# Spreading the first pair's preparation over three windows of projections, and moving the head sums ahead of the inversion's matmuls in their slot

## The chip, the cores and the metric

The kernel runs on one core of one Trainium2 chip. The metric is the device time of one execution in microseconds, the median over several runs. Times inside an execution come from one profiled run; they are counted from the start of its span.

## The reference

Two layers over 256 tokens and 2048 channels. Each layer projects the normalised input once and feeds two groups of 16 heads: a bidirectional RWKV-7 scan and windowed attention. Both are gated, joined, projected back and added to the residual. The change touches only the RWKV-7 half, whose arithmetic is, cut down:

```python
h = rms_norm(x, norm_g[l])
proj = h @ w_in[l]                       # split, and the rw part shifted between neighbours
kk = heads(kf * k_k); kk = kk * rsqrt(max(sum(kk * kk, -1), 1e-24))
for d, rev in enumerate((False, True)):
    w = -softplus(-(w0[d] + tanh(xw) @ decay_up[d])) - 0.5
    decay = exp(-exp(w))
    a = sigmoid(a0[d] + xa @ iclr_up[d])
    kd = heads(kf * (1 + (a - 1) * k_a))
    y = y + wkv_scan(rh, heads(decay), kd, vh, kk, heads(a), rev)
    bonus = bonus + sum(rh * kd * r_k, -1)
out = group_norm(y) * lnx_g + lnx_b + bonus * vh
...
x = x + concat([y_rw * silu(g_rw), y_at * silu(g_at)]) @ w_out[l]
```

## The kernel before

**Projections as a stream.** All projections of a layer are one stream of steps (class `Stream`). A step is three matmuls on TensorE (lines 286 to 288: the weights' high part with the input's high and low part, the weights' low part with the input's high part). A 128-column projection takes 16 steps. Its weights arrive in two halves by DMA, and each half is split on the fly: ScalarE writes the high part (`hi`, line 216), VectorE the low part (`lo`, line 218). The results lie in two PSUM tiles `pm` taken in turn and are evacuated by VectorE and ScalarE (lines 413 to 426).

**Windows and slots.** A layer's RWKV-7 heads are worked on in eight pairs. `window(64, ...)` runs 64 steps, the four projections of one pair (k, v, r, gate), in 14 slots of four or five steps; ahead of the steps of a slot it advances the chains of earlier pairs that are listed for that slot. Windows are counted from w = 0 in each layer, where window w projects pair w. A chain is a Python generator; one advance issues the instructions up to its next `yield`. The chains of a pair are

- `scan_p`, the preparation: low-rank products (`pza`), cumulative decay (`lw`), the sum of squares over a head (`pk`, line 654) and its reciprocal (`kd`), the scaled keys and queries (`mv`, `bk`), and the bonus `bv`, which needs a second head sum (`pbn`, line 654) over two vector operations on `lw`;
- `scan_i`, the inversion of the 64x64 blocks by doubling: masks (`pg`, line 746, then `ge`, line 752), transposes (`pt`, evacuated by ScalarE into `bt`, line 782, and four copies into `suv`, line 787), then for each level products `pq` (line 837 for the first level, 847 for the others), their evacuation `QF`, products `pd` (853, 855) and two predicated copies into `tv` and `tt` (856, 857); at the end `pf` and `pn`;
- `scan_b`, the scan over the four chunks.

In the kernel before, pair p has its preparation in window p+1, its inversion in all 14 slots of window p+2 and the first two of p+3, and its scan in p+3 and p+4. The preparation has nine parts, in slots 4 to 11 and 13 of its window, one part each. In one slot the chains are advanced in the order scan, inversion, preparation.

**What sets the order.** TensorE runs in the order of the program text (`manual_schedule`). VectorE and ScalarE get a fixed order from a planner, which puts a ready instruction by its priority: the place in the program, moved up by 40 for `lo` and by 95 for `scan_b`. Operations issued through `PA` and `PV` keep the program's order among themselves on their engine; their line in the profile is that of the helper, 231. The short-lived PSUM tiles `pza`, `pk`, `pg`, `pt`, `pq`, `pd`, `pbn`, `pf`, `pn` share one pool of two buffers of two banks each (`wpair`); a new tile takes a buffer whose last reader is done.

In the first layer `setup` also runs in window 0: it reduces the angles of the rotary positions on VectorE in a long chain (lines 340 to 359) and takes two sines on ScalarE (line 358).

Of the kernel before, what the change touches and what calls it, by code (L numbers as in the profile page):

```python
# [21 lines left out]
T = 256  # L22
# [19 lines left out]


SLOTS = 14
STAGE_P = [4, 5, 6, 7, 8, 9, 10, 11, 13]
STAGE_I = (list(range(SLOTS)), [0, 1])
STAGE_B = (list(range(1, 14)), [1, 2, 3, 4])
ATT = [
# [81 lines left out]
def hybrid_trunk_kernel(ctx, tc, xT, wi, wv, wo, par, fing, dup, iup, sink, pos, cst, out):  # L130
# [17 lines left out]
    def wpair(name):  # L148

        return ps_w.tile([128, 2, 512], F32, tag="w", name=name)  # L150

    def wbank(name):
        return wpair(name)[:, 0]

    def st(tag, shape, dt=F32, bufs=1):
        return sp.tile([128, *shape], dt, tag=tag, name=tag, bufs=bufs)
# [475 lines left out]
    def layer(l):  # L632
# [14 lines left out]
        def low_rank(o, w, x):  # L647
            PE.matmul(o, w[0], x[0], start=True, stop=False)
            PE.matmul(o, w[0], x[1], start=False, stop=False)
            PE.matmul(o, w[1], x[0], start=False, stop=True)  # L650

        def head_sums(o, x):
            for r in half:
                PE.matmul(o[r, 0:T], bones[r, r], x[r, 0:T], start=True, stop=True)
# [3 lines left out]
        def scan_p(p, t):  # L658
            K, VV, R, iu, du = t["k"], t["v"], t["r"], t["iu"], t["du"]
            dd = lambda x: x.rearrange("p (d x) -> p d x", d=2)  # L660
            two = lambda x: x.unsqueeze(1).to_broadcast([128, 2, T])
            c8 = lambda x: x.rearrange("p (n j) -> p n j", j=64)

            pza = wpair("pza")
            pz, pa = pza[:, 0], pza[:, 1]
            for d in range(2):
                low_rank(pz[:, d * T : (d + 1) * T], [a[0 : RANK + 1, d, :] for a in du], [a[0 : RANK + 1] for a in L.TW])
            LW = st("lw", [2 * T])
            for d in range(2):
                low_rank(pa[:, d * T : (d + 1) * T], [a[0:RANK, d, :] for a in iu], [a[0:RANK] for a in L.XA])  # L670
            PA.activation(LW, pz, AF.Tanh, scale=0.5)
            TH = st("th", [2 * T])
            for d in range(2):
                PA.activation(TH[:, d * T : (d + 1) * T], pa[:, d * T : (d + 1) * T], AF.Tanh, scale=0.5, bias=dpm(NSH + 16, d * 8 + p))
            sq = st("t1", [T], bufs=3)
            PA.activation(sq, K, AF.Square, scale=prm(P_KK, p))
            KR = st("kkr", [T])
            PA.activation(KR, K, AF.Identity, scale=prm(P_KK, p))
            yield

            PV.tensor_scalar(LW, LW, 1.0, None, op0=ALU.add)
            msk = MSK.rearrange("p c j -> p (c j)")
            for x in (LW[:, 0:T], LW[:, T : 2 * T][:, ::-1]):
                PV.tensor_tensor_scan(x, msk, x, 0.0, op0=ALU.mult, op1=ALU.add)
            yield
            pk = wbank("pk")
            head_sums(pk, sq)
            PP = st("pp", [2, NC, 64])
            IP = st("ip", [2, NC, 64])
            PA.activation(PP.rearrange("p d c j -> p (d c j)"), LW, AF.Exp, scale=DECAY_C)  # L690
            PA.activation(IP.rearrange("p d c j -> p (d c j)"), LW, AF.Exp, scale=-DECAY_C)
            KD = st("kd", [T])
            PV.reciprocal(KD, pk[:, 0:T])
            PV.scalar_tensor_tensor(KD, KD, 1e24, KR, op0=ALU.min, op1=ALU.mult)
            yield

            MV = st("mv", [2, NC, 2, 64], bufs=3)
            BK = st("bk", [2, NC, 3, 64])
            km = st("lw", [2 * T])
            kr4 = KR.rearrange("p (c j) -> p c j", j=64)  # L700
            PV.scalar_tensor_tensor(MV[:, 0, :, 0, 1:64], PP[:, 0, :, 0:63], -1.0, kr4[:, :, 1:64], op0=ALU.mult, op1=ALU.mult)
            PV.scalar_tensor_tensor(MV[:, 1, :, 0, 0:63], PP[:, 1, :, 1:64], -1.0, kr4[:, :, 0:63], op0=ALU.mult, op1=ALU.mult)
            PA.activation(MV[:, 0, :, 0, 0:1], kr4[:, :, 0:1], AF.Copy, scale=-1.0)
            PA.activation(MV[:, 1, :, 0, 63:64], kr4[:, :, 63:64], AF.Copy, scale=-1.0)
            PA.activation(km, TH, AF.Identity, scale=dpm(NSH, p), bias=dpm(NSH + 8, p))
            yield
            PV.scalar_tensor_tensor(dd(TH), dd(TH), 1.0, two(KD), op0=ALU.add, op1=ALU.mult)
            BK8 = BK.rearrange("p d c s j -> p (d c) s j")
            IP8 = IP.rearrange("p d c j -> p (d c) j")
            PV.scalar_tensor_tensor(BK8[:, :, 1, :], c8(TH), 0.5, IP8, op0=ALU.mult, op1=ALU.mult)  # L710
            yield
            PV.tensor_tensor(dd(km), dd(km), two(K), op=ALU.mult)
            PV.tensor_tensor(BK8[:, :, 2, :], c8(km), IP8, op=ALU.mult)
            PA.activation(BK8[64:128, :, 0, :], BK8[64:128, :, 2, :], AF.Copy)
            yield
            PV.tensor_tensor(
                MV[:, :, :, 1, :], R.rearrange("p (c j) -> p c j", j=64).unsqueeze(1).to_broadcast([128, 2, NC, 64]), PP, op=ALU.mult
            )
            PC = st("pc", [2, NC], bufs=3)
            PA.activation(PC[:, 0, :], PP[:, 0, :, 63], AF.Copy)  # L720
            PA.activation(PC[:, 1, :], PP[:, 1, :, 0], AF.Copy)
            yield


            PV.tensor_tensor(km[:, 0:T], km[:, 0:T], km[:, T : 2 * T], op=ALU.add)
            PV.scalar_tensor_tensor(km[:, 0:T], km[:, 0:T], prm(P_RK, p), R, op0=ALU.mult, op1=ALU.mult)
            yield
            pb = wbank("pbn")
            head_sums(pb, km)
            bv = st("bv", [T], bufs=3)  # L730
            PV.tensor_tensor(bv, pb[:, 0:T], VV, op=ALU.mult)
            t.update(BK=BK, MV=MV, PC=PC, bv=bv)
            yield


# [230 lines left out]
        def scans(w):  # L966

            gens = []
            for lag, scan, at in ((4, scan_b, STAGE_B[1]), (3, scan_i, STAGE_I[1]), (3, scan_b, STAGE_B[0]), (2, scan_i, STAGE_I[0]), (1, scan_p, STAGE_P)):
                p = w - lag  # L970
                if 0 <= p < NP:
                    if (scan, p) not in chains:
                        chains[scan, p] = scan(p, L.ts[p])
                    gens.append((chains[scan, p], at))
            return gens
# [73 lines left out]
        for w in range(NP + 2):  # L1049
            window(64, *scans(w), *([(setup_, [2, 5])] if l == 0 and w == 0 else []))  # L1050
        att = attend()
        window(64, *scans(NP + 2), (att, ATT[0]))
        window(64, *scans(NP + 3), (att, ATT[1]))
        window(64, (att, ATT[2]))
        for _ in att:
# [124 lines left out]
```

## Time and profile before

| | |
|---|---|
| median of 3 runs | 1224.29 us (1222.6 to 1225.03) |
| the profiled execution | 1220.4 us, of which its span 1218.6 us |
| TensorE (PE) busy | 1177.0 us, 97% of the span |
| VectorE (DVE) busy | 929.5 us, 76% |
| ScalarE (ACT) busy | 747.6 us, 61% |
| GpSimd (POOL) busy | 19.1 us, 2% |
| DMA | 166.72 MB, mean 137 GB/s |
| mean granted TensorE clock | 0.992 of full speed |

A busy share is an average over stages with different limits. The line "waits" of an engine tells how long it stood still and which engine's instruction let it go on; a row of the timeline has the start, the length, engine, line and tiles of an instruction or of a run of equal ones, and in brackets the idle time ahead of it. In a table by stretches each row has the length of a stretch, each engine's busy time in it with the count of instructions, the granted clock (PEclk, 1.00 is full speed), the DMA share and GB/s.

In layer 0, window 0 starts at 27.8 us, window 1 at 50.4, window 2 at 85.1 and window 3 at 122.3; in layer 1 they start at 623.8, 646.4, 679.8 and 716.9. Windows 4 to 7 take 42.1 us each in both layers.

### The profile page before, as it was taken

To read this page: it belongs to the slowest core of one execution; us is meant where nothing else is said; L and a number is where in the kernel's file an instruction comes from. 1 tells how busy PE (TensorE), PEld (TensorE's weight loads), DVE (VectorE), ACT (ScalarE), POOL (GpSimd) and SP (SyncE) were. 2 spreads that over 40 slices of the span, in tenths; PEclk is the share of its full clock that TensorE was granted. 3 is DMA by queue.
4 is the path that set the end of the run, shared out by engine and by line. 5 is a ranking of instruction groups with operands and counts; after the bars stand their busy time and mean duration, and the time that the engine had idled before them with its cause. 6 is when DMAs were issued, how large, how long until landed. Compare 5 with 4: busy or idle time off the path is not lost. (4 is left out here: it accounts for less than half of the span.)

```text
span 1218.6 us, 38161 instructions
## 1 busy us (share of the span) xinstructions
PE 1177.0 (97%) x16204; PEld 1092.3 (90%) x16204; DVE 929.5 (76%) x2067; ACT 747.6 (61%) x1840; POOL 19.1 (2%) x23
## 2 busy tenths in 40 slices
PE   7989999999999999999999899999999999999996
PEld 6978998999898889999999788989999888899996
DVE  7978878888877668866677788878887866786554
ACT  6656665766666557655555556766676565675553
POOL 0000000000000000000000000000000000000000
PEclk9999999999999999999999999999999999999998
DMA  7533233323323433477654333233233334345653
GB/s 252 177 129 125 95 112 111 107 96 116 119 89 102 134 111 132 141 242 237 205 189 163 111 121 114 86 107 126 90 112 106 115 101 133 125 142 177 208 191 123
DMA packets 60411, 166.72 MB, mean 137 GB/s; under 512 B 7728, under 2 KB 22736, under 8 KB 60240
## 3 DMA queue, kind: packets, MB, share of 16 engines
q1 hardware_dynamic: 60240, 164.27, 40.5%
q8 instruction: 127, 2.08, 0.7%
q14 instruction: 44, 0.36, 0.1%
HBM read 157.43 MB, written 4.19 MB: 133 GB/s over the span
## 5 line engine op out<-in xcount | busy, mean ns | idle before, releaser
L286 PE MATMUL pm<-XH,hi 128*128 128x256 f32 x1664 | 497.0, 299 | 8.1 <-ACT XH L179 5.9
L216 ACT ACTIVATE hi<-raw 128x512 fp32r<-128x512 f32 x560 | 328.4, 624 | 247.8 <-PE pm L287 173.6
L288 PE MATMUL pm<-XH,lo 128*128 128x256 f32 x1664 | 470.1, 282 | 3.2 <-DVE lo L218 3.2
L287 PE MATMUL pm<-XL,hi 128*128 128x256 f32 x1664 | 469.7, 282 | 0.1
L218 DVE TENSOR_TENSOR lo<-raw,hi 128x512 fp32r<-128x512 f32 x560 | 368.5, 687 | 89.8 <-ACT hi L216 83.0
L286 PEld LDWEIGHTS pm<-XH,hi 128*128 128x128 f32 x1664 | 315.7, 190 | 33.8 <-issue 13.4
L288 PEld LDWEIGHTS pm<-XH,lo 128*128 128x128 f32 x1664 | 316.2, 190 | 4.5 <-DVE lo L218 4.0
L287 PEld LDWEIGHTS pm<-XL,hi 128*128 128x128 f32 x1664 | 316.5, 190 | 0.7 <-DVE XL L180 0.7
L286 PE MATMUL pm<-MH,hi 128*128 128x256 f32 x512 | 144.0, 281 | 0.0
L287 PE MATMUL pm<-ML,hi 128*128 128x256 f32 x512 | 143.8, 281 | 0.0
L288 PE MATMUL pm<-MH,lo 128*128 128x256 f32 x512 | 143.8, 281 | 0.0
L286 PEld LDWEIGHTS pm<-MH,hi 128*128 128x128 f32 x512 | 96.6, 189 | 0.8 <-issue 0.8
L287 PEld LDWEIGHTS pm<-ML,hi 128*128 128x128 f32 x512 | 96.6, 189 | 0.0
L288 PEld LDWEIGHTS pm<-MH,lo 128*128 128x128 f32 x512 | 96.6, 189 | 0.0
L920 ACT ACTIVATE suv<-pcc 64x128 f32<-64x128 f32 x128 | 34.2, 267 | 20.4 <-PE pq L847 14.4
L856 DVE CAST_PREDICATED tv<-LV,pd 128x256 f16<-128x256 uint8 x80 | 34.5, 431 | 13.6 <-PE pd L855 13.1
L849 ACT ACTIVATE QF<-pq 128x256 f16<-128x256 f32 x80 | 30.9, 386 | 20.8 <-PE pq L847 20.0
L752 DVE TENSOR_TENSOR ge<-pg,C 128x1024 f32<-128x1024 f32 x32 | 39.1, 1222 | 5.0 <-PE pg L746 5.0
L904 ACT ACTIVATE rh<-pcc 128x128 f32<-128x128 f32 x64 | 17.5, 273 | 35.3 <-PE pcc L902 34.9
L1005 ACT ACTIVATE mv<-mv,mx 128x257 f32<-128x257 f32 x64 | 31.8, 502 | 11.6 <-DVE mx L1002 11.6
L746 PE MATMUL pg<-mv,bk 64*128 64x128 f32 x512 | 37.2, 285 | 0.0
L857 DVE CAST_PREDICATED tt<-LV,pd 128x256 f16<-128x256 uint8 x80 | 34.1, 426 | 0.0
(240 smaller groups left out, 1849.9 us busy)
## 6 DMA issues: line engine op xcount, KB each, us to landing
raw<-wi SPq DMA_DIRECT2D x207, 512.0 KB, 3.4
raw<-wo SPq DMA_DIRECT2D x64, 512.0 KB, 3.8
raw<-wv SPq DMA_DIRECT2D x8, 512.0 KB, 3.2
rrot<-u SPq DMA_DIRECT2D x80, 32.0 KB, 1.9
vg<-xT SPq DMA_DIRECT2D x16, 128.0 KB, 5.2
xd<-vg SPq DMA_DIRECT2D x16, 128.0 KB, 2.4
vg<-xd SPq DMA_DIRECT2D x16, 128.0 KB, 3.5
g<-dup SPq DMA_DIRECT2D x16, 97.0 KB
```

The source lines that it names most:

```text
L216: A.activation(hi[:, q], raw[:, q], AF.Copy)
L218: V.tensor_tensor(lo[:, q], raw[:, q], hi[:, q].bitcast(F32), op=ALU.subtract)
L286: PE.matmul(pm, wh, rh[:, kk, :], start=(kk == 0), stop=False)
L287: PE.matmul(pm, wh, rl[:, kk, :], start=False, stop=False)
L288: PE.matmul(pm, wl, rh[:, kk, :], start=False, stop=(kk == 15))
L746: PE.matmul(pg[:, h, c * 128 : (c + 1) * 128], BK[half[h], d, c, 1 - h : 3 - h, :].rearrange("p s j -> p (s j)"), MV[half[h], d, c].rearra ...
L752: V.tensor_tensor(GEd(d), pg.rearrange("p h (c x) -> p h c x", c=NC), gm[d].unsqueeze(1).unsqueeze(1).to_broadcast([128, 2, NC, 128]), op= ...
L849: A.activation(t_sub(QF), flat4(pq[:, :, 0:128]), AF.Copy)
L856: V.copy_predicated(t_sub(TC), t_mask, flat4(pd[:, :, 0:128]))
L857: V.copy_predicated(v_sub(TT), v_mask, flat4(pd[:, 0, 128:384].rearrange("p (d x) -> p d x", d=2)))
L920: A.activation(here(h), pc[half[h], 1], AF.Copy)
L1005: A.activation(Sc[:, h, q, 0:257], Sc[:, h, q, 0:257], AF.Exp, scale=0.125, bias=mx[:, q : q + 1], accum_out=den[:, q : q + 1])
```

## The change

The preparation gets two more `yield`s, one behind each of its head sums, and so has eleven parts: part 3 is the sum `pk` alone, part 10 the sum `pbn` alone; `BK`, `MV` and `PC` are handed on behind part 8, and `bv` behind part 11.

For pairs 1 to 7 parts 3 and 10 are advanced in slots 6 and 13 ahead of the inversion's part of the same slot, all others in the slots as before behind it. The set of instructions in each slot is the same as before.

For pair 0 the parts are spread: 1 and 2 in slots 12 and 13 of window 0; part 3 in slot 3 of window 1, 4 in slot 3 behind it, 5, 6, 7, 8 in slots 5, 6, 8, 10; part 9 in slot 1 of window 2, part 10 in slot 3 ahead of the inversion's first `pq`, and part 11 (`bv`) in slot 3 behind it.

```diff
-STAGE_P = [4, 5, 6, 7, 8, 9, 10, 11, 13]
+STAGE_P = (([6, 13], [4, 5, 6, 7, 8, 9, 10, 11, 13]),)
+STAGE_P0 = (([], [12, 13]), ([3], [3, 5, 6, 8, 10]), ([3], [1, 3]))
...
             pk = wbank("pk")
             head_sums(pk, sq)
+            yield
...
+            t.update(BK=BK, MV=MV, PC=PC)
             yield
...
             pb = wbank("pbn")
             head_sums(pb, km)
-            bv = st("bv", [T], bufs=3)
+            yield
+            t["bv"] = bv = st("bv", [T], bufs=3)
             PV.tensor_tensor(bv, pb[:, 0:T], VV, op=ALU.mult)
-            t.update(BK=BK, MV=MV, PC=PC, bv=bv)
             yield
...
-            for lag, scan, at in ((4, scan_b, STAGE_B[1]), (3, scan_i, STAGE_I[1]), (3, scan_b, STAGE_B[0]), (2, scan_i, STAGE_I[0]), (1, scan_p, STAGE_P)):
+            prep = [(lag, at) for lag, at in enumerate(STAGE_P0) if lag == w] + [(1, at) for at in STAGE_P if w > 1]
+            stages = [(4, scan_b, STAGE_B[1]), (3, scan_i, STAGE_I[1]), (3, scan_b, STAGE_B[0])]
+            stages += [(lag, scan_p, at[0]) for lag, at in prep]
+            stages += [(2, scan_i, STAGE_I[0])]
+            stages += [(lag, scan_p, at[1]) for lag, at in prep]
+            for lag, scan, at in stages:
```

## The prediction

> **What bounds the kernel now.** I read the page's busy shares first, then TensorE's list of waits, then the timeline at the longest wait, then tables by stretches.
>
> ```profile
> PE 1177.0 (97%) x16204; PEld 1092.3 (90%) x16204; DVE 929.5 (76%) x2067; ACT 747.6 (61%) x1840; POOL 19.1 (2%) x23
> ...
> PE pbn L654 <- DVE lw L231: 8.2, 2, 4.1
> PE pq L847 <- DVE tv L856: 5.8, 4, 1.6
> PE pk L654 <- ACT t L231: 1.6, 1, 1.6
> ...
> 758.60:800.60 42.00, 41.92 (x756) 38.08 (x754) 35.13 (x75) 28.08 (x74) 1.01 (x1) 1.00 0.32 107
> ```
>
> TensorE is the bound: 97% busy, and in a full window (window 4 of layer 1, the last row) 41.92 of 42.00 us. Work taken off VectorE or ScalarE there is worth nothing; only TensorE's waits can be won. The longest group is the second head sum `pbn` behind the two vector operations on `lw`: two waits of 4.1 us, one in each layer. The only `pk` wait is 1.6 us. The timeline shows where the first `pbn` wait lies and what follows it.
>
> ```profile
> 79.94 0.65 PE L654 MATMUL pbn<-lw,C 64*64 64x256 f32 x4 [4.11 <-DVE lw L231]
> 80.52 0.51 PE L286 MATMUL pm<-XH,hi 128*128 128x256 f32 x1
> ...
> 83.60 0.41 PE L288 MATMUL pm<-XH,lo 128*128 128x256 f32 x1
> ...
> 85.52 0.28 PE L286 MATMUL pm<-XH,hi 128*128 128x256 f32 x1
> 85.64 0.28 PE L287 MATMUL pm<-XL,hi 128*128 128x256 f32 x1
> ...
> 27.80:50.40 22.60, 22.60 (x192) 22.60 (x193) 20.58 (x51) 13.11 (x26) 0.00 (x0) 1.00 0.54 183
> 50.40:62.00 11.60, 11.15 (x95) 10.94 (x93) 9.77 (x25) 10.75 (x16) 0.00 (x0) 1.00 0.48 148
> 62.00:75.80 13.80, 12.65 (x100) 11.80 (x100) 13.42 (x24) 10.07 (x22) 0.00 (x0) 1.00 0.46 156
> 75.80:79.90 4.10, 0.03 (x1) 0.00 (x0) 3.92 (x9) 1.47 (x5) 0.00 (x0) 1.00 0.51 156
> 79.90:84.00 4.10, 4.07 (x21) 3.49 (x21) 0.42 (x1) 0.11 (x1) 0.00 (x0) 0.59 0.28 111
> 84.00:94.00 10.00, 10.00 (x129) 9.17 (x129) 6.68 (x12) 6.07 (x13) 0.00 (x0) 1.00 0.27 87
> ...
> 646.40:674.60 28.20, 23.40 (x195) 22.48 (x193) 23.37 (x43) 16.34 (x35) 0.00 (x0) 1.00 0.49 161
> 674.60:679.70 5.10, 5.07 (x35) 4.13 (x35) 1.20 (x3) 1.01 (x2) 0.00 (x0) 0.67 0.23 81
> ```
>
> Both `pbn` waits lie at slot 13 of window 1, where pair 0 is prepared and no inversion lengthens the window. VectorE is then the slow engine: 13.42 of 13.8 us busy ahead of the wait and 3.92 of 4.1 in it. The wait has a second price. Behind it 14 matmul starts take 83.60 - 80.52 = 3.08 us, 0.22 each, where 0.12 is the pace later (85.52 to 85.64); the granted clock is 0.59 for 4.1 us. Lost: 4.1 x 0.41 = 1.7 us. In layer 1 the clock is 0.67 for 5.1 us: 5.1 x 0.33 = 1.7 again. So each `pbn` wait costs 4.1 + 1.7 = 5.8 us. The 1.6 us `pk` wait lies in the stretch 62.0 to 75.8, whose clock is 1.00: it costs only itself.
>
> **The change part by part.** No instruction is added or removed on any engine. No moved part issues a DMA or a GpSimd instruction, so SP's and POOL's queues keep their work.
>
> *What goes.* In window 1, `pk` comes a whole window part after its squares (made in slot 12 of window 0): its wait goes, -1.6. `pbn` moves to slot 3 of window 2, two slots behind the two operations it waits for, which lie in slot 1 at VectorE's head: -5.8 in each layer. Sum: -13.2 us.
>
> *Moved low-rank products.* The twelve `pza` matmuls move from window 1 to window 0 and cost TensorE the same in either place. Their inputs are made between slots 0 and 9 of window 0, so I price a new wait at nothing; if that cover went, the price would be that of the `pk` wait, 1.6.
>
> *The new wait in window 2.* This is the one cost that the rows of the kernel before already show.
>
> ```profile
> 92.23 0.33 PE L837 MATMUL pq<-tv,AB 64*64 64x32 f16 x10
> ...
> 87.87 1.23 DVE L752 TENSOR_TENSOR ge<-pg,C 128x1024 f32<-128x1024 f32 x1 [0.56 <-PE pg L746]
> ...
> 90.44 1.15 ACT L216 ACTIVATE hi<-raw 128x512 fp32r<-128x512 f32 x2
> 91.50 0.79 ACT L782 ACTIVATE bt<-pt 128x768 f32<-128x768 f32 x1
> 92.30 1.55 ACT L787 ACTIVATE suv<-pt 64x256 f32<-64x256 f32 x4
> ...
> 182.87 0.63 PE L654 MATMUL pk<-t,C 64*64 64x256 f32 x4
> ...
> L231 DVE SCALAR_TENSOR_TENSOR lw<-lw,PR,kr 128x256 f32<-128x256 f32 x16 | 7.8, 485 | 0.6
> L231 DVE TENSOR_TENSOR lw<-lw 128x256 f32<-128x256 f32 x16 | 6.7, 420 | 0.0
> L231 DVE TENSOR_TENSOR bv<-pbn,vg 128x256 f32<-128x256 f32 x16 | 6.7, 420 | 2.1 <-PE pbn L654 2.1
> ```
>
> Today the first `pq` of pair 0 starts at 92.23, in the buffer that the second `pg` left. After the change `pbn` takes that buffer, and `pq` needs one of two others: that of `pt`, free when the last `suv` copy ends (92.30 + 1.55 = 93.85), or `pbn`'s own, free after `bv`. A head sum takes about 0.6 us (the `pk` row), so TensorE stands ready for `pq` at 92.23 + 0.6 = 92.8. Through `pt` the wait is 1.0 us; through `bv` it is 0.42 plus handing over, some 0.5. If the two `lw` operations (0.42 + 0.49) slip ahead of the second mask `ge`, the copies behind it come 0.9 later: 1.9. So 0.5 to 1.9; I take 1.0, the value with today's order, in each layer: +2.0. Queued behind the waiting `pq` are the window's steps. The second lateness of this chain follows at 115.51:
>
> ```profile
> 115.51 0.30 PE L847 MATMUL pq<-tv,AB 64*64 64x32 f16 x16 [1.63 <-DVE tv L856]
> ```
>
> There TensorE waits for VectorE's backlog, which a TensorE one microsecond later would shorten. I leave it as it is, and count up to 1.6 per layer as a possible gain.
>
> *VectorE's reserve in layer 0.* With the waits gone TensorE covers 27.8 to 79.9 (52.1 us) in 52.1 - 4.1 - 1.6 = 46.4. VectorE's work there is 20.58 + 9.77 + 13.42 + 3.92 = 47.7 us, less the 0.9 that moves to window 2. So in layer 0 it hardly keeps up, and some 2 to 3 us of splits and evacuations go over into window 2. There 84.0 to 94.0 holds 6.68 of 10.0 us of work and gets 0.42 + 0.49 + 0.42 = 1.3 more: 6.7 + 1.3 + 2.5 = 10.5 in 10. I put the cost at +1.0, between 0 and 2.6 (47.7 + 1.3 - 46.4, all of it on the path). In layer 1 no setup runs; VectorE has 23.37 of 28.2 busy in window 1, and I charge nothing.
>
> *The head sums in the other windows.*
>
> ```profile
> 185.79 0.30 PE L853 MATMUL pd<-QF,tt 64*64 64x32 f16 x16
> ...
> 184.51 1.76 DVE L231 RECIPROCAL kd<-pk 128x256 f32<-128x256 f32 x1
> ...
> 203.87 0.42 DVE L857 CAST_PREDICATED tt<-LV,pd 128x256 f16<-128x256 uint8 x1
> 204.20 0.42 DVE L231 TENSOR_TENSOR bv<-pbn,vg 128x256 f32<-128x256 f32 x1
> ...
> 204.34 0.30 PE L863 MATMUL pf<-tv,NEYE 64*64 64x256 f16 x4
> ```
>
> An earlier `pk` gives nothing: it ends at 183.50, and the reciprocal starts only at 184.51, when VectorE comes to it. What it could cost is a buffer. The reciprocal ends at 186.27, 0.48 after the next `pd` starts at 185.79; `bv` ends at 204.62, 0.28 after `pf` starts. If `pd` and `pf` must now take the head sums' buffers, a window loses 0.48 + 0.28 = 0.76 us. If they take the buffer of the `pq` or `pd` that they follow, which they wait for in any case, nothing. In the program of the kernel before, a tile takes whichever buffer is free, and one `pd` takes the one that its own `pq` has just left. So 0 to 0.76 per window; I take 0.
>
> *Sum:* -13.2 + 2.0 + 1.0 = -10.2 us. The profiled execution (1220.4, span 1218.6) would come to 1210.2; against the median shown, 1224.29 (3.9 above that execution), I predict 1214.1.
>
> **A rule that speaks against the change.** In layer 0 the moved part's tanh comes close to the setup's two sines on ScalarE.
>
> ```profile
> 51.66 1.28 ACT L358 ACT_TABLE_LOAD   x1
> 52.95 0.42 ACT L358 ACTIVATE SIN<-SIN 128x256 f32<-128x256 f32 x1
> ```
>
> A table load takes 1.28 us here, the sine starting 1.29 after it. ScalarE is busy 10.75 of 11.6 us in that stretch, so each extra change of tables would reach TensorE through late `hi` splits. If the planner sets the tanh among the sines, two more changes cost 2 x 1.29 = 2.6 us: 1214.1 + 2.6 = 1216.7.
>
> The Trainium skill, ScalarE: Activation LUTs, What ACT_TABLE_LOAD costs, puts a switch at 1283 ns of load and some 1380 ns of drain. The trace agrees on the load and shows no drain between load and sine; by the page two switches would be 5.3 us and the time 1219.4.
>
> **The rivals.**
>
> *VectorE keeps the pace.* The stalls leave window 1 and come back in part at `pg` and `pq` of window 2: the reserve costs 2.6, the new wait 1.9 in both layers. -13.2 + 3.8 + 2.6 = -6.8: 1217.5. For it: 47.7 us of work in 46.4. Against: layer 1 has room.
>
> *The reorder takes it back.* The head sums' buffers hold `pd` and `pf` in all fourteen windows of pairs 1 to 7: 14 x 0.76 = +10.6 on -10.2: 1224.7, no change. For it: only two buffers, both overtakings are in the rows above. Against: another buffer is always free by then.
>
> *Slower.* As before, but the new plan also sets the reciprocal one split later:
>
> ```profile
> L218 DVE TENSOR_TENSOR lo<-raw,hi 128x512 fp32r<-128x512 f32 x560 | 368.5, 687 | 89.8 <-ACT hi L216 83.0
> ```
>
> 14 x (0.76 + 0.69) = +20.3: 1224.3 - 10.2 + 20.3 = 1234.4. It decides from 10.2 / 14 = 0.73 us per window on. Against: it needs a wrong buffer and a worse order at once, in a stage that now has no wait.
>
> **How the numbers follow.** Forecast 0.57, tables 0.05, VectorE's pace 0.18, taken back 0.10, slower 0.10. A change under 0.2% (2.4 us) can't be told from none. Faster 0.57 + 0.05 + 0.18 = 0.80, same 0.10, slower 0.10. The range starts at 1209: -13.2, the new waits at 0.5 each (+1.0) and both 115.51 waits gone (-3.2) give -15.4, 1208.9. It ends at 1221, above the VectorE and table cases, leaving out the last two. The forecast's own range is 1209 to 1217.
>
> **What would show it.** Right: no `pbn` or `pk` wait over 0.3 us, a clock of 1.00 in window 1 of both layers, a new wait of 0.5 to 1.9 us at line 837 in window 2, and full windows still at 42 us. Wrong: waits at `pg` in layer 0 of over 2 us, waits of `pd` for the reciprocal or of `pf` for `bv`, or full windows of over 42.5 us.

## Result and the profile after

| | before | after |
|---|---|---|
| median | 1224.49 us (1222.6 to 1225.03) | 1215.89 us (1214.87 to 1218.23) |
| ratio | | 0.9935, 95% interval 0.9917 to 0.9953 |
| the profiled execution | 1220.4 us, span 1218.6 | 1214.87 us, span 1213.1 |

The change makes the kernel 8.6 us faster by the medians; predicted were 10.2 us and 1214.1 us. (The median before has one run more here than in the table ahead of the prediction, 1224.29 us.) Line numbers of the changed kernel are two to four higher: the head sums are line 656, the first `pq` 841, the later ones 851.

The page's busy shares of the changed kernel, and three of the larger groups of its TensorE waits (total, count, longest):

```profile
PE 1175.4 (97%) x16204; PEld 1096.0 (90%) x16204; DVE 928.4 (77%) x2067; ACT 747.5 (62%) x1840; POOL 19.1 (2%) x23
...
PE pq L851 <- DVE tv L860: 5.6, 5, 1.6
PE pm L290 <- DVE lo L220: 4.2, 6, 1.3
PE pq L841 <- ACT suv L791: 3.3, 2, 2.2
```

The work is the same. The `pbn` and `pk` waits are gone, and a new group stands there: the first `pq` of pair 0 waiting for the copies out of `pt`, once in each layer. The table by stretches (length, PE, PEld, DVE, ACT, POOL, then clock) shows where the time went:

```profile
28.10:52.20 24.10, 24.08 (x204) 24.08 (x205) 22.14 (x55) 14.98 (x31) 0.00 (x0) 1.00 0.52 176
52.20:78.00 25.80, 24.40 (x200) 23.10 (x198) 23.18 (x49) 18.51 (x35) 0.00 (x0) 1.00 0.46 160
78.00:89.10 11.10, 8.87 (x104) 7.74 (x104) 8.12 (x14) 7.63 (x14) 0.00 (x0) 1.00 0.44 145
645.50:669.00 23.50, 23.50 (x200) 22.85 (x198) 20.90 (x40) 14.40 (x31) 0.00 (x0) 1.00 0.55 184
...
758.60:800.60 42.00, 41.92 (x760) 38.42 (x758) 35.12 (x75) 28.00 (x74) 1.01 (x1) 1.00 0.33 107
```

Window 1 of layer 1 (645.5 on) now has TensorE busy throughout at full clock, where it stood 4.8 us before. In layer 0 it still loses 1.4 us (24.40 of 25.80 busy). The full window is as before, 41.92 of 42.00. By the first projection matmul of each window, windows 0 and 1 together shrink from 57.3 to 50.9 us in layer 0 and from 55.9 to 48.7 in layer 1, and window 2 grows from 37.2 to 40.0 and 40.4.

### The profile page after: what moved, and what is told of

Its sections match the earlier page's. It is cut to its first block, busy times and chain, and to the rows that moved or that the text cites. A ratio compares the mean times of both kernels' runs of the same rounds, so it can differ in the third digit from the quotient of the medians.

```text
span 1213.1 us, 38155 instructions
## 1 busy us (share of the span) xinstructions
PE 1175.4 (97%) x16204; PEld 1096.0 (90%) x16204; DVE 928.4 (77%) x2067; ACT 747.5 (62%) x1840; POOL 19.1 (2%) x23
## 5 line engine op out<-in xcount | busy, mean ns | idle before, releaser
L851 PE MATMUL pq<-tv,AB 64*64 64x32 f16 x1280 | 33.6, 186 | 6.4 <-DVE tv L860 5.6
L750 PE MATMUL pg<-mv,bk 64*128 64x128 f32 x512 | 37.2, 285 | 0.0
```

What stands on the lines that cost most here:

```text
L750: PE.matmul(pg[:, h, c * 128 : (c + 1) * 128], BK[half[h], d, c, 1 - h : 3 - h, :].rearrange("p s j -> p (s j)"), MV[half[h], d, c].rearra ...
L851: PE.matmul(narrow(pq[:, d], h ^ d, c), hq(AB, d, c, h), sub(TC, h, d, c, d * b), start=True, stop=True)
```

## Experiments

All times are medians; they were taken in three sets, each beside the kernel before. It had 1223.2 us beside the first three runs below and the bank of its own, 1224.1 beside the two windows, the sum in slot 0, the run without the angles and the first run with raised copies, and 1222.4 beside the last two. Runs of different sets are compared by their ratios.

**The changed kernel once more.** No edit.

> The changed kernel once more, beside the others on the same chip, so that differences of 1 to 3 us can be read. Every theory expects 1213 to 1218 us, 6 to 11 us below the kernel before. On the clock: the theory that one 3.4 us stretch of the clock's grid, about half idle, is enough to halve the clock expects the 1.6 us waits at the later pq (window 2 and window 9) to be followed by a 0.5 stretch in some executions and not in others, by where they fall; the theory that only an idle time of over 3.4 us does it expects no 0.5 stretch between 20 and 1200 us in any execution without a wait that long.

Measured: 1215.47 us, ratio 0.993 (0.9918 to 0.9942). As expected in time. On the clock the second theory falls: this profile has half clock for 3.41 us from 90.9 and from 995.5 us, each behind a stretch with 2.1 and 1.9 us of idle time and no longer wait. The last section has more.

**The order in the slot alone.**

```diff
-prep = [(lag, at) for lag, at in enumerate(STAGE_P0) if lag == w] + [(1, at) for at in STAGE_P if w > 1]
+prep = [(1, at) for at in STAGE_P]
```

> Pair 0's preparation stays whole in window 1 (slots 4 to 11 and 13, as before); only the order in the slot is changed, head sums ahead of the inversion. Main theory (the gain is the spreading of pair 0): 1224.5 us, within 2 us of the kernel before, both pbn waits of 4.1 us still there with a clock of 0.5 behind each, full windows at 42.0 to 42.1 us. Rival (the order in the slot is worth something in the full windows): 1218 or less, full windows below 41.8. Second rival (the order costs through the shared buffers, 0.76 us a window): 1235.

Measured: 1224.51 us, ratio 1.0003 (0.9993 to 1.0013). Its TensorE waits and a full window:

```profile
PE pbn L656 <- DVE lw L233: 8.2, 2, 4.1
...
758.60:800.60 42.00, 41.92 (x756) 38.41 (x756) 35.14 (x75) 28.12 (x73) 1.01 (x1) 1.00 0.32 107
```

Both long waits stand as before, and the full window is the same to 0.01 us. The order is worth nothing, and the buffers take nothing for it.

**The spreading alone.**

```diff
-STAGE_P = (([6, 13], [4, 5, 6, 7, 8, 9, 10, 11, 13]),)
+STAGE_P = (([], [4, 5, 6, 6, 7, 8, 9, 10, 11, 13, 13]),)
```

> Pair 0 is spread over three windows as in the changed kernel; pairs 1 to 7 keep their head sums behind the inversion's part of the slot, as before. Main theory: the same as the changed kernel, 1215.9 us, within 1.5 us; the pf wait at the start of window 9 in layer 0 back from 0.8 to 0.4 us. Rival (half of the gain is the order): 1220.

Measured: 1215.72 us, ratio 0.9934 (0.9921 to 0.9947). All of the gain is the spreading of pair 0. The `pf` wait is 0.54 us here and 0.45 with the order alone, and 0.78 and 1.43 in the two profiles of the changed kernel, so it doesn't follow the order.

**Two windows instead of three.**

```diff
-STAGE_P0 = (([], [12, 13]), ([3], [3, 5, 6, 8, 10]), ([3], [1, 3]))
+STAGE_P0 = (([], []), ([6], [4, 5, 6, 7, 8, 9, 10]), ([3], [1, 3]))
```

> Pair 0's parts 1 to 8 stay in window 1 (slots 4 to 10, the first head sum ahead in slot 6); only the bonus, parts 9 to 11, moves to window 2 as in the changed kernel. It tells whether the early start in window 0 is needed. Theory A (the bonus sum's late inputs were the whole trouble): the pbn waits and the half clock behind them are gone, the pk wait of 1.4 to 1.6 us in layer 0 is back, the pq waits of 2.2 and 1.0 us in window 2 stay: 1217.5 us. Theory B (VectorE is the slow engine of window 1, so the lateness only moves on): pg in window 2 waits for mv or bk by 1 to 3 us in layer 0 and under 1 in layer 1: 1219 to 1221.

Measured: 1216.86 us, ratio 0.9939 (0.9925 to 0.9952). Its waits:

```profile
PE pq L841 <- ACT suv L791: 2.6, 2, 1.3
...
PE pk L656 <- ACT t L233: 1.4, 1, 1.4
...
89.07 0.21 PE L841 MATMUL pq<-tv,AB 64*64 64x32 f16 x3 [1.30 <-ACT suv L791]
```

Theory A: no `pbn` wait, no `pg` wait, the `pk` wait back. Moving only the bonus, three of eleven parts, gives nearly all of the gain. The early start in window 0 is worth 0.5 to 1.1 us by the ratios (0.9939 against 0.9935 and 0.993), which the intervals don't separate. VectorE's lateness did not move on to `pg`. One part of theory A missed: the `pq` waits are 1.3 us in both layers, not 2.2 and 1.0. So the longer wait of layer 0 comes only with the early start; by the first projection matmul windows 0 and 1 of layer 0 take 50.9 us with it and without it, those of layer 1 48.7 and 49.5.

**A bank of its own for the moved sum.**

```diff
-pb = wbank("pbn")
+pb = ps_c.tile([128, 512], F32, tag="y", name="pbn") if p == 0 else wbank("pbn")
```

> As the changed kernel, but the second head sum of pair 0 is written to a PSUM bank that the scan uses only from window 3 on, so that the first pq of the inversion finds the buffer of the second pg free. Main theory (that pq waits for the copies out of pt only since pbn took its buffer: 2.2 us in layer 0 and 1.0 in layer 1): no wait over 0.3 us at line 841, 3.2 us less, 1212.7 us; if the later waits for tv grow in turn, 1214. Rival (pq waits for the mask and the ScalarE copies AB behind it, whatever the buffer): the waits stay and the time too, 1215.9.

Measured: 1210.28 us, ratio 0.9893 (0.9879 to 0.9908). The first groups of its waits, in order of size:

```profile
PE pm L288 <- ACT XH L181: 6.6, 1, 6.6
PE pq L851 <- DVE tv L860: 6.3, 5, 1.6
PE pm L290 <- DVE lo L220: 3.1, 6, 1.0
PE pm L288 <- ACT hi L218: 2.3, 2, 1.7
```

No wait is left at line 841, so the buffer was its cause. The gain over the changed kernel, 5.2 us, is 2 us more than the 3.3 us of waits, and more than was expected. In two of three profiles with the 2.2 us wait (the changed kernel again, and the spreading alone) a half-clock stretch stood behind it; the last section shows one. That the other 2 us lie there is not shown: the profile with the bank of its own has three half-clock stretches between 20 and 1190 us, those of the changed kernel two each.

**The moved sum in slot 0.**

```diff
-STAGE_P0 = (([], [12, 13]), ([3], [3, 5, 6, 8, 10]), ([3], [1, 3]))
+STAGE_P0 = (([], [12, 13]), ([3], [3, 5, 6, 8, 10, 12]), ([0], [0]))
```

> As the changed kernel, but pair 0's part 9 lies in slot 12 of window 1 and its second head sum in slot 0 of window 2 ahead of pg, bv behind it. Theory (the pq wait is a matter of which PSUM buffer pbn takes): pq waits under 0.3 us at line 841; pbn may wait up to 1 us in layer 0, where VectorE is late, and 0 in layer 1: 1211 to 1213 us. Rival (pbn so early meets VectorE's lateness again): pbn waits 2 us or more in layer 0 and pg's second half waits for bv: 1216 or more.

Measured: 1217.82 us, ratio 0.9954 (0.9937 to 0.9971).

```profile
PE pbn L656 <- DVE lw L233: 3.6, 2, 2.6
```

Line 841 waits no more, as the theory had it, but the rival is right on `pbn` and on the time: `pbn` waits 2.6 us in layer 0 and 1.0 in layer 1. The rival's wait of `pg` for `bv` does not show. The sum stands two slots behind its two operations here too (slot 12 to slot 0; slot 1 to slot 3 in the changed kernel), so the distance alone does not do it: at the end of window 1 the sum stands behind VectorE again. It wants a place where VectorE has had time and a free buffer at once.

**Without the rotary angles in layer 0.** The sine and cosine tables are set to constants.

```diff
-        ang = st("g", [T], bufs=2)
-        ...
-        V.tensor_scalar(SIN, SIN, C[:, C_OFF["sgn"] : C_OFF["sgn"] + 1], None, op0=ALU.mult)
+        V.memset(SIN, 0.0)
+        V.memset(COS, 1.0)
```

> The changed kernel without the first layer's chain of rotary angles: the sine and cosine tables are set to constants, so the attention half computes something else. It tells what VectorE's and ScalarE's load by that chain costs in layer 0. Theory (layer 0 loses by VectorE's lack of reserve and by table loads): in layer 0 the waits for hi and lo in window 1 (1.4 us together) go and the first pq wait falls from 2.2 to the 1.0 us of layer 1, windows 0 to 2 of both layers get within 0.7 us of each other: about 2.6 us less than the changed kernel, 1213. Rival (the layers differ by something else): under 1 us less, pq wait still over 2.

Measured: 1210.74 us, ratio 0.9895 (0.988 to 0.9911). The first `pq` of layer 0 (its line numbers are 20 lower here):

```profile
85.70 0.33 PE L821 MATMUL pq<-tv,AB 64*64 64x32 f16 x11 [1.01 <-ACT suv L771]
```

The wait is that of layer 1 to 0.01 us, and no wait for `hi` or `lo` over 0.3 us is left in window 1. Those two account for 2.6 us. The medians differ by 4.7, the ratios by 4.3; the other 2 us are not settled. With the chain on VectorE this run also loses the two sines and the four table loads in layer 0, so it does not tell these apart.

**Copies ahead of the splits.** The bank of its own, and the first predicated copy of a level raised in priority. Then the same with the head sums of pairs 1 to 7 behind the inversion, and the raised copies alone on the kernel before.

```diff
-V.copy_predicated(t_sub(TC), t_mask, flat4(pd[:, :, 0:128]))
+with tc.high_priority(offset=60):
+    V.copy_predicated(t_sub(TC), t_mask, flat4(pd[:, :, 0:128]))
```

> The kernel with a bank of its own for pair 0's second head sum, and in all windows the first predicated copy of each level (into tv) is moved up by 60 in the planner's priorities, ahead of the lo splits (40). Theory (the 1.6 us waits at the later pq in window 2 come from VectorE's order, where the copy stands behind five operations that could wait): these waits fall under 0.5 us in both layers and with them the half-clock stretch that follows some of them: 3 to 6 us less than without, 1205 to 1207. Rival (VectorE is simply full there): the waits turn up at the lo splits (line 290) and the time stays within 1.5 us of 1210.3.

> As the kernel with the bank of its own and the raised copies, but pairs 1 to 7 have their head sums behind the inversion's part of the slot again, as before the change. Theory (with the copies raised, the order is no longer free: the pbn wait of 1.6 us in window 2 now holds up the last pd behind it): the pbn waits fall to about 1.0 in both layers, 1 to 2 us less than 1205.5. Rival (VectorE's two operations on lw are what is late, the order does not matter): pbn waits 1.3 or more and the time within 1 us of 1205.5.

> The kernel before with only the raised priority (60) of the first predicated copy of each level; pair 0's preparation stays whole in window 1. Theory (the copy's place and pair 0's preparation are separate losses): the pq waits of 1.6 us in windows 2 and 9 fall under 0.6, the two pbn waits of 4.1 us stay with half clock behind them: 4 to 6 us less than before, about 1219. Rival (the copies only gain because window 1 no longer stalls): within 1.5 us of the kernel before.

Measured: 1205.51 us (ratio 0.9845, 0.9827 to 0.9863), 1203.15 us (0.9844, 0.9829 to 0.986) and 1216.68 us (0.9959, 0.9943 to 0.9974). The `pbn` waits of the first two, and a full window of the first:

```profile
112.80 0.43 PE L656 MATMUL pbn<-lw,C 64*64 64x256 f32 x2 [1.58 <-DVE lw L233]
112.82 0.23 PE L857 MATMUL pd<-QF,tt 64*64 64x32 f16 x4
...
112.78 0.43 PE L656 MATMUL pbn<-lw,C 64*64 64x256 f32 x2 [1.00 <-DVE lw L233]
...
758.60:800.60 42.00, 42.00 (x758) 38.50 (x757) 35.26 (x75) 28.18 (x75) 1.01 (x1) 1.00 0.33 109
```

The waits for `tv` in window 2 came from VectorE's order: with the copy raised they are gone, and even the full window's last 0.08 us of waiting goes. But in window 2 `pbn` of pair 1 waits in their place, 1.6 us in each layer, and by the first projection matmul window 2 of layer 0 takes 37.9 us with the raised copies and without. What falls between these two profiles are the full windows, from 42.05 to 41.85 us (about 2 us over windows 3 to 7 of both layers), and the half-clock stretches between 20 and 1190 us, from three to none. The head sum ahead of `pd` waits 1.58 us, against 1.00 behind it; a cost in time is not shown, since in the ratios the two can't be told apart. By the ratios raised copies alone take 5.0 us off the kernel before, and 5.9 off the kernel with the bank of its own: the two losses are separate. These two versions, at 1203 to 1206 us, beat both kernels.

## Why the prediction was right, and where its sizes were off

*What goes.* Predicted -13.2. Windows 0 and 1 shrank by 6.4 + 7.2 = 13.6 us, of which the two moved `pbn` sums are about 1.2; 1.4 us of new waits lie in layer 0. So 13.6 - 1.2 + 1.4 = 13.8 us went. The half clock behind the long waits, 1.7 us each, was part of it: neither window 1 shows one any more.

*The new wait in window 2.* Predicted 1.0 in each layer through `pt`, bounds 0.5 to 1.9. In layer 1 the copies end at 677.31 + 1.55 = 678.86 and `pq` starts:

```profile
677.31 1.55 ACT L791 ACTIVATE suv<-pt 64x256 f32<-64x256 f32 x4
...
678.90 0.33 PE L841 MATMUL pq<-tv,AB 64*64 64x32 f16 x11 [1.01 <-ACT suv L791]
```

The cause was priced rightly, as the bank of its own shows. In layer 0 the wait is 2.24 us, above the bound:

```profile
79.39 0.42 DVE L426 TENSOR_TENSOR g<-pm,rb 128x256 f32<-128x256 f32 x1
79.89 1.28 ACT L427 ACT_TABLE_LOAD   x1 [0.57 <-DVE g L426]
81.18 0.42 ACT L427 ACTIVATE g<-g 128x256 f32<-128x256 f32 x1
...
81.63 0.42 DVE L428 SCALAR_TENSOR_TENSOR vg<-g 128x256 f32<-128x256 f32 x1 [0.62 <-ACT g L427]
81.97 2.35 DVE L756 TENSOR_TENSOR ge<-pg,C 128x1024 f32<-128x1024 f32 x2
...
89.12 0.33 PE L841 MATMUL pq<-tv,AB 64*64 64x32 f16 x11 [2.24 <-ACT suv L791]
...
669.21 0.41 DVE L426 TENSOR_TENSOR g<-pm,rb 128x256 f32<-128x256 f32 x1
...
677.24 0.65 PE L656 MATMUL pbn<-lw,C 64*64 64x256 f32 x4
```

The last table load behind the setup's sines, which stood ahead of `pza`'s tanh, now falls in front of a gate's tanh at 79.89. VectorE waits 0.62 us for that gate, and the two masks queue behind it on VectorE, then the copies behind the masks on ScalarE. Without that wait the masks would end 0.62 us earlier at most (an estimate from these rows), which is half of the 1.2 us by which layer 0 waits longer. VectorE was also late before the load: its evacuation `g` starts 8.03 us ahead of `pbn` in layer 1 (669.21 to 677.24), but only 6.83 in layer 0 (79.39 to 86.22). Besides the one at 0.73 us the count of loads stayed at four, so the rival of two more loads did not happen; but its mechanism, a load in the way of a chain, did in part.

*VectorE's reserve in layer 0.* This term was mis-sized: predicted 1.0, bound 2.6. Measured are 1.4 us of waits for `hi` and `lo` in window 1, the longest two of them

```profile
53.14 0.39 PE L290 MATMUL pm<-XH,lo 128*128 128x256 f32 x1 [0.50 <-DVE lo L220]
68.81 0.39 PE L288 MATMUL pm<-XH,hi 128*128 128x256 f32 x1 [0.67 <-ACT hi L218]
...
68.79 0.69 DVE L220 TENSOR_TENSOR lo<-raw,hi 128x512 fp32r<-128x512 f32 x1 [1.89 <-ACT hi L218]
```

and the 2.24 - 1.01 = 1.2 by which `pq` waits longer than in layer 1, 2.6 together. That this meets the bound is luck. The bound counts the two `lw` operations (0.9 us) twice, in the 47.7 and in the 1.3; and 47.7 - 0.9 = 46.8 against 46.4 leaves 0.4 us over, not 2 to 3. Nor is all of the 2.6 VectorE's: 0.62 of it is the wait for the table load, and beside the wait for `hi` at 68.81 VectorE itself had been idle for 1.89 us; what held that split up is not settled. The two windows keep the angles and have none of the 2.6, but the `pk` wait of 1.4 instead. So in layer 0 the 1.6 us won by moving `pk` came back as other waits.

*The head sums elsewhere.* Predicted 0, between 0 and 0.76 a window: 0, by the run with the order alone. Both rivals built on it are out.

*The later `pq` waits.* Left as they were, and so they are: 1.63 us in each layer before, 0.34 + 1.24 and 1.64 after.

*The sum.* -13.8 + 2.24 + 1.01 + 1.4 = -9.15 us, against 8.6 by the medians; one half clock more or less, 1.7 us, is larger than the difference. The two profiled spans differ by only 5.5 us: the changed kernel's has two half-clock stretches, in window 2 and window 9 of layer 1, which the sum leaves out. The prediction priced half clock only behind the 4.1 us waits. That the 1.6 us `pk` wait cost only itself holds for that wait, but carrying it over to the other short waits was wrong: in this profile 1.64 us of idle time in window 2 of layer 1 had half clock behind it, and so had the later wait in window 9. Of the rivals, VectorE keeping the pace came in part: the measured 1215.9 lies about halfway between its 1217.5 and the forecast, but no wait at `pg` shows, and layer 1 has the forecast's 1.01.

## What to carry to other kernels

Find the one place where an in-order engine waits for a chain, and move the end of the chain to where the slow engine has had time for it; here three of eleven parts gave nearly all of the gain. When a result moves ahead in a pool of two buffers, name the tile that now takes the other buffer and price its last reader. A wait's price includes the clock behind it, and here waits of 1.6 us, half of the clock's 3.41 us stretch, had one too in some executions.

## What the runs showed of the hardware

Within each of the twelve profiles, the changes of the granted clock lie whole multiples of 3.41 us apart: the clock goes in stretches of 3.41 us on a grid, which lies elsewhere in each execution. I had taken half clock to follow only the long waits. The stretches of the grid with a wait, each with the one behind it, for the changed kernel, the kernel before, the spreading alone and the two windows:

```profile
699.30:702.70 3.40, 1.76 (x29) 1.63 (x28) 3.40 (x8) 1.23 (x3) 0.00 (x0) 1.00 0.59 178
702.70:706.10 3.40, 3.40 (x21) 3.04 (x22) 2.26 (x5) 1.43 (x3) 0.00 (x0) 0.50 0.36 133
...
708.70:712.10 3.40, 1.89 (x30) 1.86 (x30) 3.10 (x9) 1.22 (x4) 0.00 (x0) 1.00 0.60 224
712.10:715.50 3.40, 3.40 (x64) 2.75 (x66) 2.25 (x6) 0.56 (x2) 0.00 (x0) 1.00 0.38 131
...
86.70:90.10 3.40, 1.17 (x25) 0.80 (x22) 1.41 (x3) 2.55 (x6) 0.00 (x0) 1.00 0.41 119
90.10:93.50 3.40, 3.40 (x32) 3.14 (x31) 2.34 (x7) 1.64 (x4) 0.00 (x0) 0.50 0.14 57
...
87.20:90.60 3.40, 2.10 (x31) 1.69 (x32) 1.33 (x4) 1.78 (x5) 0.00 (x0) 1.00 0.61 218
90.60:94.00 3.40, 3.40 (x43) 3.24 (x42) 2.96 (x6) 2.54 (x6) 0.00 (x0) 1.00 0.12 20
```

TensorE busy 1.76 of 3.40 us is followed by half clock, 1.89 and 2.10 are not, 1.17 is. Over the twelve profiles, between 20 and 1187 us and counting stretches that ran at full clock themselves, those with under 1.5 us of idle time were never followed by half clock, those with over 1.8 us always (12 of 12), those with 1.52 to 1.64 us in 10 of 18. Two stretches outside this count fit less well: one at 1190.2 us, in the version with the head sums behind, had half clock behind it after 1.32 us idle, and one already at half clock, with the order alone, had a second behind it after 0.52 us. So about half a stretch of idle time can be enough, and what a wait costs depends in part on where it falls on the grid: the 1.64 us wait of the changed kernel lies whole in its stretch, while its 2.24 us wait in layer 0 was cut into 1.46 and 0.78 by the grid and had no half clock behind it. The place is not all: with the sum in slot 0 a stretch with 1.64 us idle kept the clock, and what decides between 1.52 and 1.64 us is not settled. The version with the bank and the raised copies has no half clock between 20 and 1190 us.

The Trainium skill, TensorE: Matmul & The Clock Gate, Part 1, has windows of 3413 ns that run free of the kernel's start, the clock falling after an idle window of about 3.4 us, and advises against idle gaps longer than that. The grid and its length agree with the trace; the condition does not, as 1.76 us busy in the stretch was not enough to keep the clock.
